# A gated recurrence on TensorE: diagonal chunk scores as whole 128 by 128 products, or as 32 by 32 blocks

## The chip, the cores and the metric

The kernel runs on one core of a Trainium2 chip. The core has a matrix engine (TensorE, "PE" in the profile, with its weight loads shown apart as "PEld"), a vector engine (DVE), an activation engine (ACT), a general engine (POOL) and a queue engine that issues transfers (SP). They run side by side and wait for one another through semaphores. SBUF is the working memory, with 128 partitions; PSUM is the memory that TensorE writes, also with 128 partitions, from which DVE and ACT copy out.

The metric is the device time of one execution in microseconds. Less is better.

## The reference

Two layers of a decoder trunk over 1024 positions of width 1024, in float32. Layer 0 mixes positions by sliding-window attention, layer 1 by a gated linear recurrence with 8 heads of key width 128 and value width 128. The change is in layer 1 alone. There, with a query `qi`, a key `ki`, a value `vi` and a log forget gate `gi` for each position and head, and chunks of 32 positions:

```python
def step(S, inp):
    qi, ki, vi, gi = inp
    b = jnp.cumsum(gi, axis=2)
    b_last = b[:, :, -1:, :]
    o_inter = jnp.einsum('bhck,bhkv->bhcv', qi * jnp.exp(b), S)
    diff = b[:, :, :, None, :] - b[:, :, None, :, :]
    decay = jnp.exp(jnp.where(causal, diff, -jnp.inf))
    scores = jnp.einsum('bhtk,bhtsk->bhts', qi, decay * ki[:, :, None, :, :])
    o_intra = jnp.einsum('bhts,bhsv->bhtv', scores, vi)
    S_new = S * jnp.exp(b_last)[:, :, 0, :, None] + jnp.einsum(
        'bhck,bhcv->bhkv', ki * jnp.exp(b_last - b), vi)
    return S_new, o_inter + o_intra
```

A query position sees the keys of its own chunk up to itself, each decayed by the gates between the two, and everything older through the state `S`. Before the recurrence a projection makes q, f (the gate) and the values, after it comes a norm, a second gate z and an output projection.

## The kernel before

The kernel doesn't keep the reference's chunk of 32. It treats 128 positions at a time, so there are 8 chunks a head, and builds a score matrix `sc` of 128 keys (on the partitions) by 128 queries for each chunk. The state is carried from chunk to chunk only. `scores_block(h, Q, F, K)` makes the scores of one head, with arrays of 128 features on the partitions and 1024 positions along the row:

- L753 to L781 prepare, on DVE and POOL: two scans (L757, L758) make running products of the gates inside blocks of 16 positions; from them come `U` and `V`, the queries and keys scaled so that their product within a block of 32 positions is right, and `X` and `Y` (the arrays Q and K themselves, further scaled) for the parts off the diagonal.
- L783 to L788 make the diagonal parts. For each of the 8 chunks TensorE multiplies all 128 keys of `V` by all 128 queries of `U`, four chunks in one PSUM tile of tag "s". A copy with a mask (L788) then takes over, out of each 128 by 128 product, only the four 32 by 32 blocks on the diagonal and of these only the keys that are not later than the query. `sc` was set to zero once, by `zeros`, so the rest stays zero.
- L789 to L797 make the parts between neighbouring blocks of 32: 16 matmuls of 32 keys by 32 queries, whose outputs stand at partitions 0 to 31 and 64 to 95 of one more PSUM tile, and two copies on ACT.
- L798 to L810 scale `X` and `Y` further (L802 on DVE, L803 on POOL) and make the parts between the two halves of a chunk: 8 matmuls of 64 by 64, and one copy on ACT.

`rec(h)` calls it and goes on: transposes of `Y` (L824), the state's increments (L830) and its update on DVE (L834, L836), then the outputs `sc` times values (L843) and queries times state (L845).

Everything in float32 leaves two records on TensorE for each matmul of the program. The big products of the projections go through `product` (L189), which makes three passes over operands that have been split into a high and a low part; their weights come from HBM through `fetch` and are split on ACT (L154) and DVE (L155) as buffers come free (`advance`, `used`).

The order of the units is `plan` in `mixer1` (L873, L874): the projections for head h+1 or h+2 stand before the recurrence of head h, so that TensorE has them to do while DVE and POOL prepare the scores. The order of the instructions on each engine is then laid out when the program is built, by a scheduler that follows an estimated time line (L1037), so the work of a head may be cut and interleaved with that of its neighbours. PSUM tiles of one tag share two buffers (`pp`, L100). `scs` holds two score matrices, one for even and one for odd heads. The other form, `scores_tree`, is for gates that are too small; it is not run with these inputs.

Of the kernel before, what the change touches and what calls it, by code (L numbers as in the profile page):

```python
# [12 lines left out]
F32 = mybir.dt.float32  # L13
# [10 lines left out]
P = 128  # L24
# [30 lines left out]
M_L, M_D, M_N = 2 * P, 2 * P + 7 * 64, 3 * P + 7 * 64  # L55
# [34 lines left out]
def emit(tc, I, out):  # L90
    nc = tc.nc
    v = InOrder(tc, nc.vector)
    from contextlib import ExitStack
    top = ExitStack()
    with top:
# [4 lines left out]
        pp = top.enter_context(tc.tile_pool(name="ps", bufs=2, space=PSUM))  # L100
# [7 lines left out]
        msk = const.tile([P, M_L], U8, name="msk")  # L108
# [557 lines left out]
        def mixer1(fast, vo, rp):  # L666
# [6 lines left out]
            msk = rp.tile([P, M_N - M_L], U8, name="msk")  # L673
# [74 lines left out]
            def scores_block(h, Q, F, K):  # L748


                sc = scs[h % 2]

                v.tensor_copy(F1[:, ::16], F[:, :T:16])  # L753
                nc.gpsimd.memset(F[:, :T:16], 0.0)
                U = rp.tile([P, T], F32, tag="U", name="U")
                V = rp.tile([P, T], F32, tag="V", name="V")
                v.tensor_tensor_scan(U, F[:, :T], F1, 0.0, op0=ALU.mult, op1=ALU.add)  # L757
                v.tensor_tensor_scan(V[:, ::-1], F[:, T:0:-1], E1[:, ::-1], 0.0, op0=ALU.mult, op1=ALU.add)  # L758
                v.tensor_tensor(Q, Q, U, op=ALU.mult)
                v.tensor_tensor(K, K, V, op=ALU.mult)  # L760

                def blk(a, n):
                    return a.rearrange("p (b two n) -> p b two n", two=2, n=n)

                tt = rp.tile([P, 6, 32], F32, tag="tt", bufs=2, name="tt")
                t32, t64, t128 = tt[:, 4, :], tt[:, 5, :16], tt[:, 5, 16:24]
                e1, e2, r1, r2 = (tt[:, i, :].unsqueeze(2).to_broadcast([P, 32, 16]) for i in range(4))
                for i in range(2):
                    v.tensor_copy(tt[:, i, :], U[:, 16 * i + 15::32])
                v.reciprocal(tt[:, 2:4, :], tt[:, 0:2, :])  # L770
                v.tensor_tensor(t32, tt[:, 0, :], tt[:, 1, :], op=ALU.mult)
                for a, b in ((t64, t32), (t128, t64)):
                    bv = b.rearrange("p (b two) -> p b two", two=2)
                    v.tensor_tensor(a, bv[:, :, 0], bv[:, :, 1], op=ALU.mult)
                Q2, K2, M2, N2 = blk(Q, 16), blk(K, 16), blk(U, 16), blk(V, 16)
                v.tensor_tensor(M2[:, :, 0, :], Q2[:, :, 0, :], r1, op=ALU.mult)
                nc.gpsimd.tensor_copy(M2[:, :, 1, :], Q2[:, :, 1, :])
                nc.gpsimd.tensor_copy(N2[:, :, 0, :], K2[:, :, 0, :])
                v.tensor_tensor(N2[:, :, 1, :], K2[:, :, 1, :], r2, op=ALU.mult)
                v.tensor_tensor(Q2[:, :, 1, :], Q2[:, :, 1, :], e1, op=ALU.mult)  # L780
                nc.gpsimd.tensor_tensor(K2[:, :, 0, :], K2[:, :, 0, :], e2, op=ALU.mult)  # L781
                X, Y = Q, K
                for b4 in range(2):  # L783
                    ps = pp.tile([P, 4, P], F32, tag="s", name="pss")
                    for i in range(4):
                        cs = slice((b4 * 4 + i) * P, (b4 * 4 + i + 1) * P)
                        nc.tensor.matmul(ps[:, i, :], V[:, cs], U[:, cs], start=True, stop=True)  # L787
                    v.copy_predicated(sc[:, b4 * 4:b4 * 4 + 4, :], msk[:, M_D - M_L:].unsqueeze(1).to_broadcast([P, 4, P]), ps)  # L788
                ps = pp.tile([P, 8, 64], F32, tag="s", name="pss")  # L789
                for c in range(8):  # L790
                    for j in range(2):
                        o = c * P + 64 * j
                        nc.tensor.matmul(ps[64 * j:64 * j + 32, c, :32], Y[:, o:o + 32], X[:, o + 32:o + 64],  # L793
                                         start=True, stop=True)
                for j in range(2):
                    o = 64 * j
                    nc.scalar.activation(sc[o:o + 32, :, o + 32:o + 64], ps[o:o + 32, :, :32], AF.Copy)  # L797
                for n, tot in ((32, t32), (64, t64)):  # L798
                    Xv, Yv = blk(X, n), blk(Y, n)
                    nb = T // (2 * n)  # L800
                    tv = tot.rearrange("p (b two) -> p b two", two=2)
                    v.tensor_tensor(Xv[:, :, 1, :], Xv[:, :, 1, :], tv[:, :, 0:1].to_broadcast([P, nb, n]), op=ALU.mult)  # L802
                    nc.gpsimd.tensor_tensor(Yv[:, :, 0, :], Yv[:, :, 0, :], tv[:, :, 1:2].to_broadcast([P, nb, n]),  # L803
                                            op=ALU.mult)
                    if n == 32:
                        ps = pp.tile([P, 8, 64], F32, tag="s", name="pss")
                        for c in range(8):
                            nc.tensor.matmul(ps[:64, c, :], Y[:, c * P:c * P + 64], X[:, c * P + 64:(c + 1) * P],  # L808
                                             start=True, stop=True)
                        nc.scalar.activation(sc[:64, :, 64:], ps[:64], AF.Copy)  # L810
                return sc, X, Y, t128

            def rec(h):
                vt = vo[h // 4]
                hc = slice((h % 4) * P, (h % 4 + 1) * P)
                ins = (qfk[h, 0], qfk[h, 1], qfk[h, 2])
                sc, X, Y, tot = scores_block(h, *ins) if fast else scores_tree(*ins)
                yn = rp.tile([P, 8, P], F32, tag="yn", name="yn")
                S = rp.tile([P, 8, P], F32, tag="S", name="S")
# [221 lines left out]
```

## Time and profile before

| What | us |
|---|---|
| median of 3 runs | 926.09 (924.61 to 927.68) |
| the profiled execution, device time | 928.78 |
| the profiled execution, span from first to last instruction | 927.0 |
| first and last start of the 128 by 128 products (L787) in it | 482.9 and 736.7 |

The profile is of one execution. A line of its groups gives the source line, the engine, the operation, the tile written and the tiles read, the shape, the count, then the time that the group was busy, the mean of one in ns, and the idle time of the engine just before. A line of its time line gives start, duration, engine, source line, operation, tiles, shape and count; neighbours of one group are merged. A line of the busy times by windows gives, for each engine, its busy time and in brackets how many instructions touch the window. For TensorE the ends of matmuls are modelled and overlap, so what one costs is read from the distance of starts.

### The profile page before, as it was taken

What the parts mean: (1) busy time and instruction counts of PE and PEld (TensorE: products, weight loads), DVE (VectorE), ACT (ScalarE), POOL (GpSimd) and SP (SyncE); (2) the same over time, 40 slices, a digit from 0 to 9 for tenths busy, and PEclk for the clock granted to TensorE, in tenths of its full rate; (3) what the DMA queues carried; (4) which work ended last, traced back from release to release, by engine and by line L of the source; (5) the groups of instructions that cost most, each with busy time, mean ns of one, the idle gap of its engine ahead of it and who ended that gap; (6) DMA issues with size and microseconds to landing.
All of it is one profiled execution on the core that took longest, in us unless ns stands there. A gap on an engine that the chain in (4) does not pass through costs nothing.

```text
span 927.0 us, 13290 instructions
## 1 busy us (share of the span) xinstructions
PE 900.5 (97%) x4830; PEld 754.3 (81%) x4830; DVE 545.9 (59%) x895; ACT 374.5 (40%) x958; POOL 350.1 (38%) x506
## 2 busy tenths in 40 slices
PE   6989999999999999999999999999999999999996
PEld 4768888888887788878888888888888888888885
DVE  6859898777885535762276864227775835252233
ACT  6425667666656332543322331323233234242211
POOL 5503455667787203330153531114433633220011
PEclk9998999999999999999999999999999999999998
DMA  7454364512312223541210010121111002022053
GB/s 283 135 154 144 109 180 141 160 55 65 92 52 60 91 67 135 176 136 37 89 58 28 20 46 1 53 62 35 35 46 47 1 1 81 11 82 101 24 181 118
DMA packets 53252, 78.56 MB, mean 85 GB/s; under 512 B 4760, under 2 KB 24984, under 8 KB 53176
## 3 DMA queue, kind: packets, MB, share of 16 engines
q1 hardware_dynamic: 53032, 77.51, 26.9%
q8 instruction: 40, 0.66, 0.3%
q14 instruction: 36, 0.29, 0.1%
q10 hardware_dynamic: 144, 0.10, 0.1%
HBM read 58.89 MB, written 16.88 MB: 82 GB/s over the span
## 4 chain that ended last, share of the span: by engine, by line
PE 76%; POOL 8%; DVE 5%; issue 5%; DMA 3%; ACT 2%; SPq 0%; POOLq 0%; ACTq 0%; DVEq 0%
PE psmm L189 62%; POOL rstd L217 2%; PE pso L843 2%; PE pss L787 2%; PE pso L845 1%; PE psk L830 1%; PE pss L514 1%; PE pss L515 1%; POOL ms L215 1%; PE pst L535 1%; POOL mY L546 1%; PE pss L808 1%; POOL mY L549 1%; DMA sinT<-csd 1%; PE pst L824 1%
## 5 line engine op out<-in xcount | busy, mean ns | idle before, releaser
L189 PE MATMUL psmm<-acth,whi 128*128 128x512 f32 x528 | 209.6, 397 | 2.0 <-DVE th L474 1.1
L189 PE MATMUL psmm<-acth,wlo 128*128 128x512 f32 x528 | 208.8, 395 | 0.2 <-POOL wlo L155 0.2
L189 PE MATMUL psmm<-actl,whi 128*128 128x512 f32 x528 | 208.6, 395 | 0.0
L189 PE MATMUL psmm<-whi,acth 128*128 128x512 f32 (+1 forms) x520 | 202.5, 391 | 1.1 <-DVE y L616 0.6
L189 PE MATMUL psmm<-wlo,acth 128*128 128x512 f32 (+1 forms) x520 | 201.3, 388 | 0.0
L189 PE MATMUL psmm<-whi,actl 128*128 128x512 f32 (+1 forms) x520 | 201.3, 388 | 0.0
L155 DVE TENSOR_TENSOR wlo<-wraw,whi 128x512 fp32r<-128x512 f32 x126 | 92.3, 745 | 108.6 <-ACT whi L154 103.7
L189 PEld LDWEIGHTS psmm<-acth,whi 128*128 128x128 f32 x528 | 99.6, 189 | 22.5 <-DVE th L474 2.2
L189 PEld LDWEIGHTS psmm<-acth,wlo 128*128 128x128 f32 x528 | 99.6, 189 | 19.8 <-POOL wlo L155 0.6
L189 PEld LDWEIGHTS psmm<-whi,acth 128*128 128x128 f32 x520 | 97.7, 188 | 21.4 <-DVE y L616 0.9
L189 PEld LDWEIGHTS psmm<-actl,whi 128*128 128x128 f32 x528 | 99.7, 189 | 18.3
L189 PEld LDWEIGHTS psmm<-whi,actl 128*128 128x128 f32 x520 | 97.7, 188 | 20.3 <-DVE actl L593 0.6
L189 PEld LDWEIGHTS psmm<-wlo,acth 128*128 128x128 f32 x520 | 97.8, 188 | 19.0
L154 ACT ACTIVATE whi<-wraw 128x512 fp32r<-128x512 f32 x112 | 70.3, 631 | 87.6 <-PE psmm L189 67.3
L529 ACT ACTIVATE sm<-sm,st 128x129 f32<-128x129 f32 x128 | 50.1, 394 | 53.4 <-DVE st L527 53.4
L698 POOL TENSOR_SCALAR gate<-gate,lbt 128x512 f32<-128x512 f32 x16 | 15.5, 970 | 127.1 <-ACT gate L696 127.1
L217 POOL TENSOR_TENSOR rstd<-ms,nhalf 128x1 f32<-128x1 f32 (+1 forms) x48 | 42.7, 889 | 3.8
L904 DVE TENSOR_TENSOR y<-psmm,wpost 128x512 f32<-128x512 f32 (+1 forms) x17 | 11.2, 660 | 52.4 <-ACT jk L903 49.7
L546 POOL TENSOR_SCALAR_AFFINE_SELECT mY<-pT 64x256 fp32r<-64x256 f32 x56 | 29.3, 523 | 32.2 <-ACT pT L538 27.1
L803 POOL TENSOR_TENSOR kk<-kk,tt 128x512 f32<-128x512 f32 x16 | 24.9, 1558 | 34.5 <-PE pss L793 28.6
L514 PE MATMUL pss<-KH,QS 128*128 128x256 f32 (+1 forms) x128 | 33.4, 288 | 3.7 <-DMA QS<-qd 3.7
L903 ACT ACTIVATE jk<-psmm 128x512 f32<-128x512 f32 (+1 forms) x17 | 9.7, 573 | 65.7 <-PE psmm L189 65.7
(225 smaller groups left out, 1465.5 us busy)
## 6 DMA issues: line engine op xcount, KB each, us to landing
wraw<-in_w SPq DMA_DIRECT2D x132, 256.0 KB
QS<-qd SPq DMA_DIRECT2D x16, 512.0 KB
xr<-in_x SPq DMA_DIRECT2D x8, 512.0 KB
x1d<-xn SPq DMA_DIRECT2D x8, 512.0 KB
xr<-x1d SPq DMA_DIRECT2D x8, 512.0 KB
out_dram<-xn SPq DMA_DIRECT2D x16, 256.0 KB
xh<-in_x SPq DMA_DIRECT2D x4, 512.0 KB
qd<-qh SPq DMA_DIRECT2D x8, 256.0 KB
```

The source lines that it names most:

```text
L154: nc.scalar.activation(hi, raw, AF.Copy)
L155: W["split_ins"][i] = (nc.gpsimd if on_pool else v).tensor_tensor(lo, raw, hi.bitcast(F32), op=ALU.subtract)
L189: nc.tensor.matmul(ps, a, b, start=(k == 0 and i == 0), stop=(k == NK - 1 and i == 2))
L217: W["rstd"] = keep(nc.gpsimd.tensor_tensor(r, m, nhalf[:, :width], op=ALU.pow))
L514: nc.tensor.matmul(ps[:, i, :nkk], q, KH[:, g, k0:k0 + nkk], start=True, stop=False)
L529: nc.scalar.activation(sm[:, h, :], sm[:, h, :], AF.Exp, bias=nm[:, h:h + 1], scale=0.125, accum_out=dn[:, h:h + 1])
L546: nc.gpsimd.affine_select(mY[r, :, :64], src[64:, :, :64].bitcast(F32), [[0, 4], [-1, 64]], ALU.is_gt, 0.0, base=0, channel_multiplier=1)
L698: nc.gpsimd.tensor_scalar(dst, dst, ol, lb, op0=ALU.mult, op1=ALU.add)
L787: nc.tensor.matmul(ps[:, i, :], V[:, cs], U[:, cs], start=True, stop=True)
L803: nc.gpsimd.tensor_tensor(Yv[:, :, 0, :], Yv[:, :, 0, :], tv[:, :, 1:2].to_broadcast([P, nb, n]), op=ALU.mult)
L843: nc.tensor.matmul(po[:, i, :], sc[:, c, :], vt[:, c, hc], start=True, stop=(c == 0))
L904: v.tensor_tensor(y[:, c0:c1], ps, wpost[:, c * 512 + c0:c * 512 + c1], op=ALU.mult)
```

## The change

The whole products of the diagonal are replaced by blocks. For each chunk `c` and each block of 32 positions at offset `o`, one matmul takes the 32 keys of `V` and the 32 queries of `U` at the same positions, and writes its 32 by 32 result to PSUM at partitions `o` to `o + 31`, in the columns of chunk `c`. All 32 results of a head fit one tile of 128 partitions by 8 by 32. Then four copies with a mask, one for each group of 32 partitions, take all 8 chunks over into `sc`.

```diff
                 X, Y = Q, K
-                for b4 in range(2):
-                    ps = pp.tile([P, 4, P], F32, tag="s", name="pss")
-                    for i in range(4):
-                        cs = slice((b4 * 4 + i) * P, (b4 * 4 + i + 1) * P)
-                        nc.tensor.matmul(ps[:, i, :], V[:, cs], U[:, cs], start=True, stop=True)
-                    v.copy_predicated(sc[:, b4 * 4:b4 * 4 + 4, :], msk[:, M_D - M_L:].unsqueeze(1).to_broadcast([P, 4, P]), ps)
+
+                ps = pp.tile([P, 8, 32], F32, tag="s", name="psd")
+                for c in range(8):
+                    for o in range(0, P, 32):
+                        cs = slice(c * P + o, c * P + o + 32)
+                        nc.tensor.matmul(ps[o:o + 32, c, :], V[:, cs], U[:, cs], start=True, stop=True)
+                for o in range(0, P, 32):
+                    r = slice(o, o + 32)
+                    mk = msk[r, M_D - M_L + o:M_D - M_L + o + 32]
+                    v.copy_predicated(sc[r, :, r], mk.unsqueeze(1).to_broadcast([32, 8, 32]), ps[r])
                 ps = pp.tile([P, 8, 64], F32, tag="s", name="pss")
```

A head has 32 matmuls where it had 8, with a quarter of the columns on either side; four masked copies of 32 by 256 where it had two of 128 by 512; and three PSUM tiles of tag "s" where it had four. The new matmuls write the tile `psd`. Everything else is as before; the lines behind it move down by four.

## The prediction

> **What bounds the kernel now.** I read the page first: the busy times, then the chain of work that ended last, by engine and by line.
>
> ```profile
> PE 900.5 (97%) x4830; PEld 754.3 (81%) x4830; DVE 545.9 (59%) x895; ACT 374.5 (40%) x958; POOL 350.1 (38%) x506
> PE 76%; POOL 8%; DVE 5%; issue 5%; DMA 3%; ACT 2%; SPq 0%; POOLq 0%; ACTq 0%; DVEq 0%
> PE psmm L189 62%; POOL rstd L217 2%; PE pso L843 2%; PE pss L787 2%; PE pso L845 1%; PE psk L830 1%; PE pss L514 1%; PE pss L515 1%; POOL ms L215 1%; PE pst L535 1%; POOL mY L546 1%; PE pss L808 1%; POOL mY L549 1%; DMA sinT<-csd 1%; PE pst L824 1%
> ```
>
> TensorE carries three quarters of that chain, and the line to be changed, L787, is 2% of it. A busy TensorE may still be waiting inside, so I asked for the stage itself: the busy times by windows through the recurrence, and the waits of PE from 419 to 836 us.
>
> ```profile
> core 0: us, PE busy (x) PEld busy (x) DVE busy (x) ACT busy (x) POOL busy (x), PEclk, DMA share, GB/s
> 480.00:520.00 40.00, 40.00 (x286) 34.15 (x285) 28.08 (x40) 12.53 (x32) 14.54 (x17) 1.00 0.17 54
> ...
> 720.00:770.00 50.00, 50.00 (x319) 42.67 (x318) 27.94 (x43) 11.30 (x34) 23.21 (x19) 1.00 0.00 1
> 770.00:836.00 66.00, 66.00 (x335) 55.43 (x335) 29.30 (x40) 26.72 (x57) 16.68 (x15) 1.00 0.22 70
> ```
>
> Between 480 and 836 us PE is busy in every microsecond, at a granted clock of 1.00. The wait view for that stretch has no row at all, and the next engine, DVE, is busy 28.08 of 40 us where it is fullest. So a microsecond that TensorE loses or gains in this stage moves the end by a microsecond, as long as nobody new makes it wait. Nothing but PE time and PE waits has to be priced.
>
> **The change part by part: the matmuls.** Each head now makes 8 whole 128 by 128 products at L787. How long such a block holds TensorE is read from the starts in the time line, because the modelled ends overlap.
>
> ```profile
> 482.41 0.39 PE L189 MATMUL psmm<-acth,whi 128*128 128x512 f32 x1
> 482.63 0.39 PE L189 MATMUL psmm<-actl,whi 128*128 128x512 f32 x1
> 482.86 0.39 PE L189 MATMUL psmm<-acth,wlo 128*128 128x512 f32 x1
> 483.09 1.95 PE L787 MATMUL pss<-U,V 128*128 128x128 f32 x16
> 484.79 0.48 PE L189 MATMUL psmm<-acth,whi 128*128 128x512 f32 x1
> 485.11 0.39 PE L189 MATMUL psmm<-actl,whi 128*128 128x512 f32 x1
> ```
>
> The 8 products are 16 records: a float32 matmul leaves two. Two plain projection slots take 482.86 - 482.41 = 0.45 us. From the last plain start before the block to the second after it are 485.11 - 482.86 = 2.25 us, so the block costs 2.25 - 0.45 = **1.80 us** a head.
>
> The new block has 4 x 8 = 32 matmuls, 64 records, each of 32 stationary columns and 32 moving columns over 128 rows. That form is already in this trace: L793 has it, 16 matmuls a head, with outputs that alternate between partitions 0 and 64.
>
> ```profile
> 489.21 0.39 PE L189 MATMUL psmm<-actl,whi 128*128 128x512 f32 x1
> 489.53 0.70 PE L793 MATMUL pss<-qf,kk 128*32 128x32 f32 x32
> 490.16 0.50 PE L189 MATMUL psmm<-acth,wlo 128*128 128x512 f32 x1
> 490.50 0.39 PE L189 MATMUL psmm<-acth,whi 128*128 128x512 f32 x1
> ...
> 496.42 0.39 PE L189 MATMUL psmm<-acth,wlo 128*128 128x512 f32 x1
> 496.73 1.15 PE L808 MATMUL pss<-qf,kk 128*64 128x64 f32 x16
> 497.81 0.50 PE L189 MATMUL psmm<-acth,whi 128*128 128x512 f32 x1
> 498.14 0.39 PE L189 MATMUL psmm<-actl,whi 128*128 128x512 f32 x1
> ```
> ```profile
> 489.52:489.55 0.03, 0.02 (x2) 0.02 (x2) 1.00 0.00 0
> L808 PE MATMUL pss<-qf,kk 128*64 128x64 f32 x128 | 9.2, 225 | 0.0
> L793 PE MATMUL pss<-qf,kk 128*32 128x32 f32 x256 | 6.1, 198 | 0.0
> ```
>
> L793's block costs 490.50 - 489.21 - 0.45 = 0.84 us. Its records start over 0.70 - 0.20 (the last one's own 198 ns) = 0.50 us, so 0.84 - 0.50 = 0.34 us is a fixed price of leaving and entering the full-width form. L808 gives the same: 1.72 - 0.45 = 1.27 us, of which 1.15 - 0.22 = 0.93 us are starts, again 0.34 us beside them. In L808 all outputs stand at the same partitions, and a record takes 0.93/15 = 62 ns for 64 columns, so 31 ns for 32, alone. In L793 a record comes every 0.50/32 = 16 ns. That is twice as often as one alone could: **the two groups of output partitions run side by side**, and the window of 30 ns at the start of the block holds two starts already.
>
> The new block goes round four groups, partitions 0, 32, 64 and 96. No row shows four at once, so its price is bounded from both sides. If all four run side by side, 64 records are 16 rounds of four at 31 ns, 0.50 us, and the block costs 0.84 us, a gain of 0.96 us a head. If never more than two run, it is 64 x 16 ns = 1.00 us, a cost of 1.34 us and a gain of 0.46 us. If none overlap, 64 x 31 ns = 1.98 us, a cost of 2.32 us and a loss of 0.52 us. I take the first, with 0.02 us for the later starts in a round: **0.94 us a head, 7.5 us for eight heads**. My reason is that a group seems to wait for nothing but its own previous record (31 ns alone, two records in 31 ns with two groups).
>
> The Trainium skill, page "TensorE: Matmul & The Clock Gate", section "Wait — 56ns, not 53.3ns?", speaks against the change: it says that matmuls never start closer than about 25 ns, however few columns they have. The 16 ns above don't agree. By that rule the block would cost 64 x 25 ns + 0.34 us = 1.94 us, 0.14 us a head more than now. Part 3 of the same page has groups of output columns starting some 4 ns apart and three of them 2.38 times as fast as one; carried over to four (estimate: 2.38/3 x 4 = 3.2 times) it would give 31/3.2 x 64 = 0.62 us, a gain of 0.84 us a head.
>
> **Cuts of the block.** The order on the engines is laid out when the program is built, and it cuts blocks where another head's work is ready. One such cut of L793 shows the price.
>
> ```profile
> 516.48 0.39 PE L845 MATMUL pso<-S,qf 128*128 128x128 f32 x2
> 516.80 0.31 PE L793 MATMUL pss<-qf,kk 128*32 128x32 f32 x6
> 517.04 0.49 PE L843 MATMUL pso<-o,sc 128*128 128x128 f32 x2
> 517.37 0.39 PE L845 MATMUL pso<-S,qf 128*128 128x128 f32 x2
> ```
>
> From 516.48 to 517.37 are 0.89 us. Two pairs of 128-column records would take 2 x 2 x 0.111 = 0.45 us (1.80/16 = 0.11 us each), and 6 records at 16 ns another 0.10 us, so the cut costs 0.34 us more, the fixed price again. The old L787 blocks are cut once in three heads (at 543, 713 and 734 us, below), and that cost nothing, because the neighbours had the same width.
>
> ```profile
> 543.41 1.56 PE pss L787 x14
> 713.66 1.56 PE pss L787 x14
> 734.33 0.81 PE pss L787 x6
> ```
>
> The same three cuts would now cost 3 x 0.34 = 1.0 us. In the first two of these heads the rest of L787 stands directly before L793; where the whole new block does, one fixed price is saved, up to 0.7 us. I take 0.5 us for both together, between 0.3 (all of it saved) and, for twice the cuts and no neighbours, 2.0.
>
> **The copies.** Two copies with a mask over 128x512 become four over 32x256.
>
> ```profile
> L522 DVE COPY_PREDICATED sm<-msk,pss 128x256 f32<-128x256 uint8 x64 | 26.8, 444 | 0.7 <-PE pss L515 0.5
> L788 DVE COPY_PREDICATED sc<-msk,pss 128x512 f32<-128x512 uint8 x16 | 11.8, 737 | 5.4 <-PE pss L787 5.4
> L797 ACT ACTIVATE sc<-pss 32x256 f32<-32x256 f32 x16 | 6.0, 372 | 21.0 <-PE pss L793 20.8
> L518 ACT ACTIVATE sm<-pss 128x256 f32<-128x256 f32 x56 | 20.0, 381 | 0.8 <-PE pss L515 0.3
> ```
>
> On ACT, 32 partitions cost the same as 128 (372 against 381 ns), so I price the new copy by the row of 128x256: 4 x 0.444 = 1.78 us against 2 x 0.737 = 1.47 us, **0.3 us more DVE time a head**, 2.4 us in all. It could be no more than 4 x 0.737 = 2.9 us. The old first copy waits for four products (8 records, 0.9 us), the new ones for all 32 matmuls (0.5 us of starts, 1.0 us if only two run at once), so they begin about when they do now, or some 0.3 us later.
>
> ```profile
> 484.33 1.49 DVE L788 COPY_PREDICATED sc<-msk,pss 128x512 f32<-128x512 uint8 x2
> 485.71 0.21 DVE L753 COPY F<-gate 128x64 f32<-128x64 f32 x1
> 486.23 2.29 DVE L757 TENSOR_TENSOR_SCAN U<-gate,F 128x1024 f32<-128x1024 f32 x1 [0.31 <-POOL gate L754]
> L843 PE MATMUL pso<-o,sc x64: 271/275/377, 515.1 to 634.6; 128*128 128x128 f32 x64
> ```
>
> Queued behind the copies on DVE is the next head's preparation (L753, L757), which TensorE needs only some 25 us later, at that head's L787 (511 us). The scores themselves are first read by L843 at 515 us. The cover is PE's projections; without it the copies would cost at most those 2.4 us. A head also takes three buffers of tag "s" in place of four, and its L793 no longer has to wait for a copy of the same head; neither was waited for, so I price that at zero. No DMA is added or moved. Work of PE that ends 7 us earlier wants its weights earlier; the DMA share is 0.00 from 720 to 770 us, because all buffers are full, so there is room.
>
> The sum: -7.5 + 0.5 = **-7.0 us**. It is made against the profiled execution, 928.78 us with a span of 927.0 us; that is 2.7 us above the median of the runs shown, and I carry the difference over to the median: 926.1 - 7.0 = **919.1 us**.
>
> **The rivals.** (1) TensorE runs only two groups at once, or looks ahead only far enough for two: 8 x 0.46 = 3.7, less 0.5, so 922.9 us; with a look-ahead between, 920 to 922. For it: two is all the trace shows. Against it: nothing in the 31 ns rounds looks full, two starts fit into 30 ns. (2) Slower: neighbouring groups exclude each other. The only pair shown, 0 and 64, isn't adjacent; the new order always steps to a neighbour, so every record would run alone: 8 x 0.52 + 0.5 = 4.7 us, 930.8 us. It decides from 1.80 - 0.34 = 1.46 us for 64 starts, 23 ns a record. (3) Each step to another group has a price of its own, so that a record comes midway between the 16 ns of two groups and the 31 ns of one alone, every 23.5 ns: 1.50 + 0.34 = 1.84 us a block, 8 x 0.04 + 0.5 = 0.8 us, 926.9 us, no change that can be told. The mean of 16 ns in L793, which changes its group at each matmul, speaks against it. The Trainium skill's floor of 25 ns ("TensorE: Matmul & The Clock Gate", "Wait — 56ns, not 53.3ns?") lies near this price; the trace goes below it. (4) The change does what it says, but the new order of the program cuts the blocks often: at 0.34 us a cut, 14 cuts eat 4.7 of the 7.5 us and leave 2.8; three are there now. That gives 923.3 us. Nothing here speaks for so many.
>
> **How the numbers follow.** My forecast has 0.58, rival 1 0.25, rival 2 0.06, rival 3 0.04, rival 4 0.07. The likeliest time is 919.1 us. The range goes from 917.0 (all four groups, no cut, neighbours joined, and a microsecond of scatter) to 924.0, past rival 1 and rival 4; it leaves out rivals 2 and 3 and some tails. About 0.3%, 2.8 us, is what a measurement of this kernel can tell from no change. Faster by more is the forecast and three quarters of rival 1, 0.76; slower by more is rival 2 and a tail of rival 3, 0.07; the rest, 0.17, is within.
>
> **What would show it.** In the changed kernel's time line the new matmuls should be 64 records a head whose starts take about 0.52 us, with PE still busy throughout 480 to 760 us. 1.0 us would be rival 1, 1.5 us rival 3, 2.0 us rival 2. More than six stretches of them beyond eight would be rival 4. The masked copies should take about 0.44 us each. I'm wrong in the premise if PE gets a wait in the recurrence, or if the last stage starts earlier and yet the end doesn't move.

## The result and the profile after

The changed kernel took 919.97 us (median of 6 runs, 919.27 to 922.27) against 926.06 us before (6 runs, 924.61 to 927.68). The ratio is 0.9938, with a 95% interval of 0.9923 to 0.9954: about 0.6%, 6.1 us, faster. Forecast were 919.1 us and a gain of 7.0 us.

From the page of the profile after, the busy times and the chain by engine:

```profile
span 917.5 us, 14082 instructions
PE 891.1 (97%) x5214; PEld 744.8 (81%) x5214; DVE 551.2 (60%) x911; ACT 373.7 (41%) x958; POOL 342.1 (37%) x506
...
PE 72%; POOL 9%; DVE 7%; issue 5%; DMA 3%; ACT 2%; SPq 0%; POOLq 0%; ACTq 0%; DVEq 0%
```

PE's busy time fell by 9.4 us and the span by 9.5 us, though the medians differ by only 6.1 us. The chains of the two traces tell the rest. First before, then after; columns are start, duration, what:

```profile
419.08 64.17 PE psmm L189 x283
483.25 1.78 PE pss L787 x16
```
```profile
415.96 64.17 PE psmm L189 x283
480.13 0.72 PE psd L788 x51
480.85 0.55 PE pss L797 x31
```

The long stretch of projections that ends at the first block of the recurrence starts 3.1 us earlier in the profile after, ahead of anything that changed. That part is scatter of the single executions (the changed kernel's own executions differ by up to 2.4 us there). From the start of this stretch to the end of the span are 927.0 - 419.08 = 507.9 us before and 917.5 - 415.96 = 501.5 us after: **6.4 us** less. I call this the tail. Two more executions of the changed kernel, profiled beside the experiments, have tails of 501.7 and 501.9 us, so it is a steadier measure than the span; it is used below beside the ratios. What scatter it has sits at its end: from the start of TensorE's last product (L189) to the end of the span are 8.6, 8.7 and 9.0 us in the three traces of the changed kernel, and as little as 8.0 us in others below. Up to that start the stage takes 918.25 - 419.08 = 499.2 us before, and 493.0, 493.1 and 493.0 us after, **6.1 to 6.2 us** less; tails that differ by about 1 us are compared by this instead.

The first block after, in PE's time line:

```profile
479.29 0.39 PE L189 MATMUL psmm<-acth,whi 128*128 128x512 f32 x1
479.51 0.39 PE L189 MATMUL psmm<-actl,whi 128*128 128x512 f32 x1
479.74 0.39 PE L189 MATMUL psmm<-acth,wlo 128*128 128x512 f32 x1
480.06 0.79 PE L788 MATMUL psd<-U,V 128*32 128x32 f32 x64
480.70 0.70 PE L797 MATMUL pss<-qf,kk 128*32 128x32 f32 x32
481.33 0.50 PE L189 MATMUL psmm<-acth,whi 128*128 128x512 f32 x1
481.66 0.40 PE L189 MATMUL psmm<-actl,whi 128*128 128x512 f32 x1
```
```profile
480.05:480.09 0.04, 0.03 (x4) 0.03 (x5) 1.00 0.00 0
```

64 records start over 0.79 - 0.20 = 0.59 us, 9 ns each. The window row under it (busy time of the new matmuls alone) holds four starts in 30 ns: all four groups of output partitions run side by side. And the neighbour blocks (now L797) follow directly, without full-width work between. Both together cost 481.66 - 479.74 - 0.45 = 1.47 us, where the old kernel paid 1.80 + 0.84 = 2.64 us in two places. I call such an unbroken run of narrow (32-column) records between full-width work a stretch.

The masked copies and the waits of PE in the recurrence, after:

```profile
L792 DVE COPY_PREDICATED sc<-msk,psd 32x256 f32<-32x256 uint8 x32 | 14.1, 442 | 7.0 <-PE psd L788 5.7 <-PE pss L797 0.8
PE psd L788 <- DVE tt L774: 0.9, 1, 0.9
PE psmm L189 <- DVE qf L690: 0.2, 1, 0.2
```

A copy takes 442 ns, as priced. The waits are new: PE had none in this stage before.

### The profile page after: what moved, and what is told of

It is laid out like the page before. It is cut to its first block, busy times and chain, and to the rows that moved or that the text cites. A ratio compares the mean times of both kernels' runs of the same rounds, so it can differ in the third digit from the quotient of the medians.

```text
span 917.5 us, 14082 instructions
## 1 busy us (share of the span) xinstructions
PE 891.1 (97%) x5214; PEld 744.8 (81%) x5214; DVE 551.2 (60%) x911; ACT 373.7 (41%) x958; POOL 342.1 (37%) x506
## 4 chain that ended last, share of the span: by engine, by line
PE 72%; POOL 9%; DVE 7%; issue 5%; DMA 3%; ACT 2%; SPq 0%; POOLq 0%; ACTq 0%; DVEq 0%
PE psmm L189 59%; POOL rstd L217 2%; PE psk L834 1%; PE pso L847 1%; PE pss L514 1%; PE pss L515 1%; POOL ms L215 1%; PE pso L849 1%; PE pst L535 1%; POOL mY L546 1%; POOL mY L549 1%; DMA sinT<-csd 1%; PE pss L812 1%; PE pst L828 1%; PE pst L861 1%
## 5 line engine op out<-in xcount | busy, mean ns | idle before, releaser
L189 PE MATMUL psmm<-acth,whi 128*128 128x512 f32 x528 | 210.0, 398 | 1.6 <-DVE th L474 1.1
L189 PE MATMUL psmm<-acth,wlo 128*128 128x512 f32 x528 | 208.1, 394 | 0.2 <-POOL wlo L155 0.2
L189 PE MATMUL psmm<-actl,whi 128*128 128x512 f32 x528 | 208.2, 394 | 0.0
L189 PE MATMUL psmm<-whi,acth 128*128 128x512 f32 (+1 forms) x520 | 202.4, 391 | 1.0 <-DVE y L616 0.6
L189 PE MATMUL psmm<-wlo,acth 128*128 128x512 f32 (+1 forms) x520 | 201.2, 388 | 0.0
L189 PE MATMUL psmm<-whi,actl 128*128 128x512 f32 (+1 forms) x520 | 201.2, 388 | 0.0
L189 PEld LDWEIGHTS psmm<-acth,whi 128*128 128x128 f32 x528 | 99.6, 189 | 21.9 <-DVE th L474 2.2
L189 PEld LDWEIGHTS psmm<-acth,wlo 128*128 128x128 f32 x528 | 99.5, 189 | 19.9 <-POOL wlo L155 0.6
L189 PEld LDWEIGHTS psmm<-whi,acth 128*128 128x128 f32 x520 | 97.7, 188 | 21.2 <-DVE th L474 0.9
L189 PEld LDWEIGHTS psmm<-actl,whi 128*128 128x128 f32 x528 | 99.7, 189 | 18.4
L189 PEld LDWEIGHTS psmm<-whi,actl 128*128 128x128 f32 x520 | 97.7, 188 | 20.3 <-DVE actl L593 0.8
L189 PEld LDWEIGHTS psmm<-wlo,acth 128*128 128x128 f32 x520 | 97.8, 188 | 19.1
L698 POOL TENSOR_SCALAR gate<-gate,lbt 128x512 f32<-128x512 f32 x16 | 17.7, 1108 | 121.8 <-ACT gate L696 121.8
L546 POOL TENSOR_SCALAR_AFFINE_SELECT mY<-pT 64x256 fp32r<-64x256 f32 x56 | 29.3, 523 | 31.8 <-ACT pT L538 26.8
L549 POOL TENSOR_SCALAR_AFFINE_SELECT mY<-pT 64x256 fp32r<-64x256 f32 x64 | 30.8, 481 | 6.0 <-ACT pT L538 1.4
```

What stands on the lines that cost most here:

```text
L189: nc.tensor.matmul(ps, a, b, start=(k == 0 and i == 0), stop=(k == NK - 1 and i == 2))
L546: nc.gpsimd.affine_select(mY[r, :, :64], src[64:, :, :64].bitcast(F32), [[0, 4], [-1, 64]], ALU.is_gt, 0.0, base=0, channel_multiplier=1)
L549: nc.gpsimd.affine_select(mY[r, :, 64:], src[:64, :, 64:].bitcast(F32), [[0, 4], [1, 64]], ALU.is_ge, 0.0, base=0, channel_multiplier=-1)
L698: nc.gpsimd.tensor_scalar(dst, dst, ol, lb, op0=ALU.mult, op1=ALU.add)
```

## The experiments

Each changes the new kernel in one place and keeps the rest.

| run | us | ratio to before | tail, us |
|---|---|---|---|
| changed kernel, again | 921.97 | 0.9938 (0.9922 to 0.9955) | 501.7 |
| group by group | 928.56 | 1.0013 (1.0003 to 1.0024) | 509.2 |
| two groups | 922.07 | 0.9952 (0.9937 to 0.9966) | 502.6 |
| blocks twice | 927.26 | 1.0000 (0.9990 to 1.0010) | 507.5 |
| copies twice | 926.92 | 0.9989 (0.9979 to 0.9998) | 507.3 |
| half the copies | 919.80 | 0.9928 (0.9907 to 0.9949) | 500.4 |
| two tiles | 929.29 | 1.0025 (1.0008 to 1.0042) | 509.8 |
| uncut | 919.61 | 0.9932 (0.9917 to 0.9948) | 501.4 |
| changed kernel, again | 922.11 | 0.9938 (0.9924 to 0.9952) | 501.9 |
| uncut, copies as before | 922.23 | 0.9948 (0.9935 to 0.9962) | 501.8 |

The kernel before had medians of 926.5 to 927.6 us beside them. In "copies twice" the chain doesn't pass through the stretch by which the tail is taken, so its start is read from PE's time line, 418.82 us there and 416.03 us in the changed kernel.

> The changed kernel once more, beside the experiments. About 920.0 us, 0.9938 of the kernel before, by every theory.

> The changed kernel once more, beside the next one. Ratio to the kernel before 0.9938, by every theory.

Both came out at 0.9938.

**Is it the rotation over groups, or the size alone?** Group by group:

```diff
-                for c in range(8):
-                    for o in range(0, P, 32):
+                for o in range(0, P, 32):
+                    for c in range(8):
```

> The same 32 matmuls a head, but all eight of one group of output partitions before the next group. Theory (groups run side by side, each waits 31 ns for its own last record): the 64 records a head take 1.0 us where the queue of TensorE reaches into the next group, up to 64 x 31.7 ns = 2.0 us where it does not, in place of 0.6 us; the kernel takes 923 to 931 us. Rival (small products are cheap by their size, the order doesn't matter): 920 us, starts over 0.6 us as before.

Its first block in PE's time line:

```profile
482.00 1.82 PE L788 MATMUL psd<-U,V 128*32 128x32 f32 x61
483.63 0.22 PE L797 MATMUL pss<-qf,kk 128*32 128x32 f32 x2
483.66 0.20 PE L788 MATMUL psd<-U,V 128*32 128x32 f32 x1
```

61 starts in 1.82 - 0.20 = 1.62 us, 27 ns each, three times as long as in the rotating order; the tail is 7.3 to 7.7 us longer, and the whole gain is gone. Size alone buys nothing. Two groups at a time:

```diff
-                for c in range(8):
-                    for o in range(0, P, 32):
+                for half in range(2):
+                    for c in range(8):
+                        for o in (32 * half, 32 * half + 64):
```

> The same 32 matmuls a head, the groups at partitions 0 and 64 first in turns, then those at 32 and 96. Stretches as in the changed kernel, 16. Theory (a group waits 31 to 32 ns for its own last record, so two groups give a record every 16 ns): 1.0 us of starts a head in place of 0.6, 8 x 0.42 = 3.4 us more than the changed kernel, ratio about 0.9975. Rival (groups are not what makes it quick): ratio 0.994, starts over 0.6 us.

```profile
481.53 0.39 PE L189 MATMUL psmm<-acth,wlo 128*128 128x512 f32 x1
481.85 1.02 PE L789 MATMUL psd<-U,V 128*32 128x32 f32 x58
482.68 0.22 PE L798 MATMUL pss<-qf,kk 128*32 128x32 f32 x2
...
483.64 0.39 PE L189 MATMUL psmm<-actl,whi 128*128 128x512 f32 x1
```

58 starts take 1.02 - 0.20 = 0.82 us, 14 ns each. With the neighbours the stretch costs 483.64 - 481.53 - 0.45 = 1.66 us against 1.47. The direction is as expected, the size is not: up to TensorE's last product 1.4 to 1.5 us more in place of 3.4. The interval of the ratio doesn't tell this run from the changed kernel; the starts do. One reason is in the rows: records of L798 start among the last ones of L789, and the trace shows the same where the second pair follows the first.

**What sets the pace of a long block?** Each block made twice:

```diff
-                for c in range(8):
+                for c in list(range(8)) * 2:
```

> Each diagonal block of a head is made twice into the same place, so 128 records a head instead of 64. In the changed kernel's trace the first 32 records or so of a block come four in 32 ns, 8 ns each, the later ones every 16 to 17 ns. Theory (the first ones stood in the queue already, later ones come as fast as instructions reach TensorE): the further 64 records cost 64 x 16.7 ns = 1.07 us a head, 8.6 us in all, and with two cuts more (0.7 us) the kernel takes 929 us. Rival (the slow end is an effect of the end of a block; the four groups alone set the pace): 64 x 8 ns = 0.51 us a head, 4.1 + 0.7 us, 925 us.

```profile
481.93 1.32 PE L788 MATMUL psd<-U,V 128*32 128x32 f32 x128
```

128 starts take 1.32 - 0.20 = 1.12 us; the second 64 cost 0.53 us here, 8 ns each. The theory of a slow supply of instructions falls; the rival's 4.8 us is near the 5.6 to 6.0 us by which the tail grew (507.5 against 501.5 to 501.9). Over all eight heads the starts grew by 5.0 us, and two more stretches make 0.7 us. I had misread the end of a block, where starts come in pairs (one or two ns apart, the next pair 15 ns later), as single starts 16 ns apart.

**Do the copies lie under TensorE's work?** Twice, and half (the copies of the groups at 64 and 96 are left out):

```diff
-                for o in range(0, P, 32):
+                for o in list(range(0, P, 32)) * 2:
                     r = slice(o, o + 32)
```

> The four masked copies of a head are made twice, 4 x 0.442 = 1.77 us more of DVE a head, 14.1 us in all. Theory (DVE's copies lie under TensorE's work): nothing but two cuts more of the narrow blocks, 0.7 us: 920 to 922 us, and TensorE still busy throughout the recurrence but for a microsecond. Rival (DVE has become the bound in the recurrence, since it is busy 31 to 33 of 40 us there): up to 934 us, with waits of TensorE on DVE.

```diff
-                for o in range(0, P, 32):
+                for o in range(0, 64, 32):
                     r = slice(o, o + 32)
```

> The masked copies of the groups at partitions 64 and 96 are left out, so half of the diagonal scores are missing; DVE has 2 x 0.442 = 0.88 us less a head, 7.1 us in all. Stretches as in the changed kernel, 16. Theory (DVE is close to its limit in the recurrence, where doubled copies cost 5 of 14 us, but the changed kernel pays for it with 1.1 us of waits at most): 0 to 1.1 us less than the changed kernel, ratio 0.9925 to 0.994. Rival (the masked copies hold TensorE up by more than the waits show): 2 to 3 us less, ratio 0.991.

Doubled, the copies cost 0.9989 - 0.9938 = 0.5%, 4.7 us by the ratio and 5.4 to 5.8 us by the tail, of the 14 us added: more than the theory, less than the rival. PE's waits on DVE and one place of its time line, copies twice:

```profile
PE psmm L189 <- DVE qf L690: 3.9, 4, 1.4
PE psd L788 <- DVE V L779: 0.7, 1, 0.7
```
```profile
526.99 0.39 PE L189 MATMUL psmm<-acth,wlo 128*128 128x512 f32 x1
528.03 0.69 DVE L690 TENSOR_TENSOR qf<-psmm,sg 128x512 f32<-128x512 f32 x1
528.77 0.50 PE L189 MATMUL psmm<-acth,whi 128*128 128x512 f32 x1 [1.40 <-DVE qf L690]
```

The projections stop because a PSUM buffer of theirs is emptied by L690 on DVE, which stands in DVE's queue behind the longer work. Halved, the copies bring 0.1%, which the intervals don't tell from nothing. The tail is 500.4 against 501.5 to 501.9 us, 1.1 to 1.5 us less, but about half of that lies behind TensorE's last product; up to it the gain is 492.4 against 493.0 to 493.1 us, 0.6 to 0.7 us. PE's waits in the recurrence, half the copies:

```profile
PE pst L828 <- POOL kk L807: 0.4, 1, 0.4
PE psmm L189 <- DVE qf L690: 0.2, 1, 0.2
```

The wait of 0.9 us for L774 is gone, and one of 0.4 us for POOL is new. DVE's part in the changed kernel is small, and it is not zero.

**What does a cut cost?** Two tiles, so that the neighbour blocks must wait for a buffer again:

```diff
+                for b4 in range(2):
+                    ps = pp.tile([P, 4, 32], F32, tag="s", name="psd")
...
-                    v.copy_predicated(sc[r, :, r], mk.unsqueeze(1).to_broadcast([32, 8, 32]), ps[r])
+                        v.copy_predicated(sc[r, b4 * 4:b4 * 4 + 4, r], mk.unsqueeze(1).to_broadcast([32, 4, 32]), ps[r])
```

> The same 32 matmuls a head, but into two PSUM tiles of four chunks each, with eight masked copies of 32x128 in place of four of 32x256, so that the neighbour blocks have to wait for a buffer again. In the program's order the narrow float32 blocks then stand in 25 stretches between full-width work, where the changed kernel has 16. Theory (each stretch costs 0.34 us of leaving and entering the full-width form, whatever is in it): 9 x 0.34 = 3.1 us more than the changed kernel, ratio to the kernel before about 0.997. Rival (the stretches cost nothing, the blocks alone set the time): the changed kernel's ratio, 0.994.

The tail grew by 8.3 us, not by 3.1. Waits of PE, the busy times by windows (the granted clock is the third figure from the end) and a piece of the time line, two tiles:

```profile
PE psd L789 <- DVE V L779: 3.4, 1, 3.4
PE pss L813 <- DVE qf L807: 0.4, 1, 0.4
```
```profile
728.20:730.83 2.63, 0.47 (x2) 0.15 (x1) 2.63 (x3) 0.59 (x1) 2.63 (x2) 1.00 0.00 0
730.84:732.04 1.20, 0.00 (x0) 0.02 (x1) 1.20 (x3) 0.00 (x0) 1.20 (x2) 0.50 0.00 0
732.05:737.65 5.60, 5.60 (x44) 4.48 (x45) 3.10 (x7) 0.00 (x0) 2.43 (x2) 0.50 0.00 0
737.67:740.00 2.33, 2.33 (x17) 1.70 (x16) 0.00 (x0) 0.00 (x0) 0.00 (x0) 1.00 0.00 0
```
```profile
734.94 0.63 PE L189 MATMUL psmm<-whi,acth 128*128 128x512 f32 x1
735.37 0.63 PE L189 MATMUL psmm<-wlo,acth 128*128 128x512 f32 x1
```

3.8 us are waits on DVE, whose eight copies cost more than four (19.0 us against 14.1 in all); the changed kernel has 1.1 us of waits itself, so this adds 2.7 us. After the long one the clock is 0.50 for 5.6 us of work, and a projection slot takes 0.43 us in place of 0.23: eleven slots of them are 2.2 us. Some 8.3 - 2.7 - 2.2 = 3.4 us are left for ten more stretches (nine of 32-column blocks, and one block of L813 is cut too), 0.34 us each. As a remainder of an experiment that did more than was meant, that would be weak; but the price also stands in the time line by itself:

```profile
639.97 0.39 PE L189 MATMUL psmm<-acth,wlo 128*128 128x512 f32 x1
640.29 0.27 PE L789 MATMUL psd<-U,V 128*32 128x32 f32 x8
640.49 0.50 PE L189 MATMUL psmm<-acth,whi 128*128 128x512 f32 x1
640.82 0.39 PE L189 MATMUL psmm<-actl,whi 128*128 128x512 f32 x1
```

From 639.97 to 640.82 are 0.85 us; less 0.45 for the two slots and 0.27 - 0.20 = 0.07 for the starts, 0.33 us remain, for a stretch of 8 records as for one of 96 (1.47 - 1.14 = 0.33 us in the changed kernel's first, where 1.14 us lie between the first start and the last). By the same reckoning each of the ten stretches before and fourteen of the sixteen after cost 0.32 to 0.33 us; PE waited in the other two.

**A version without cuts.** The diagonal and the neighbour blocks get priority:

```diff
-                ps = pp.tile([P, 8, 32], F32, tag="s", name="psd")
+                with hp():
+                    ps = pp.tile([P, 8, 32], F32, tag="s", name="psd")
...
```

> The diagonal and the neighbour blocks with their copies go ahead of other ready work, so that in the program's order all 48 narrow matmuls of a head stand in one stretch: 8 stretches in place of 16. Theory of the stretches: 8 x 0.34 = 2.7 us less than the changed kernel, and the 0.9 us wait of the last head may go or stay: ratio to the kernel before about 0.991. Rival (stretches cost nothing, or DVE's copies, now earlier, hold the next preparation up): 0.994 or more.

> As in the uncut version, all 48 narrow matmuls of a head stand in one stretch (8 stretches, the changed kernel has 16), but only the matmuls go ahead of other ready work; the masked copies keep their place. In the uncut version TensorE waited 1.1 us on DVE for the state and 1.1 us for the last head's preparation. Theory (the uncut version gave its 2 us back because the copies, ahead on DVE, held the state up): these waits go down to about 1 us, and the ratio is 0.9925 or less, 1 to 2 us below the changed kernel. Rival (the waits come from DVE being full there, wherever the copies stand): as the changed kernel, 0.993 to 0.994, with 2 us of waits.

There are 8 stretches, as meant, and neither version is measurably faster than the changed kernel. Waits of PE in the recurrence, uncut:

```profile
PE psd L789 <- DVE tt L774: 1.1, 1, 1.1
PE pso L848 <- DVE S L841: 1.1, 3, 0.6
PE psmm L189 <- DVE qf L690: 0.2, 1, 0.2
```

The second version has the same three rows with the same times, so the place of the copies is not the reason; its theory falls and the rival's time holds, while its reason, a full DVE, isn't tested by itself. By 0.34 us a stretch 2.7 us should have come. By these rows the waits grew by 1.3 us over those of the changed kernel. The modelled ends hide a part of each wait, though: read from the distances of starts, as the blocks are, PE loses about 3.3 us at them in the uncut version and 1.3 us in the changed kernel, 2.0 us more. The starts of the narrow records add 0.3 us. Some 0.4 us of gain should be left; up to TensorE's last product 492.8 us against 493.0 to 493.1 show 0.2 to 0.3 us.

## Why the prediction was right, point by point

- **TensorE bounds the stage.** Right but for 1.1 us: the tail fell with PE's work, and PE is busy throughout the recurrence but for two waits on DVE. The prediction had named any wait of PE there as a sign that its premise fails; to that extent it did.
- **The groups run side by side, four at once.** Right. This was the step without a row, and it carried the result: 0.59 us of starts against a forecast of 0.52, no other case nearer (1.0, 1.5, 2.0). The first block was 0.07 us dearer than forecast. Over all stretches the 32-column records take 9.1 us from first start to last, where the old L793 alone took 4.1, so the new matmuls take 5.0 us in place of 8 x 0.52 = 4.2: the term was 0.8 us too small. The two experiments on the order show that the rotation is the cause. The Trainium skill's floor of 25 ns between starts ("TensorE: Matmul & The Clock Gate", "Wait — 56ns, not 53.3ns?") doesn't hold here, at 9 ns; the estimate from Part 3 of that page, 0.62 us, was close.
- **Cuts.** Half right. I counted three cuts more and perhaps two joined neighbours, and "priced at zero" that L793 no longer waits for a copy of its own head. That freed buffer is what lets the neighbour blocks follow at once: the last part of every new block has L797 directly behind it, whole in seven heads and its first two records in the last one; with two tiles, which take the buffer back, that happens in one head only. Against this stand more cuts than I thought: the new matmuls are in 14 stretches, six beyond eight, just as many as the prediction allowed before it would speak of rival 4. With L797 the narrow blocks are in 16 stretches, where the old L793 alone was in 10. I had counted 8 x 0.34 us for the new blocks and 0.5 us for cuts and joins, 3.2 us; six more stretches at 0.33 us are 2.0 us, 1.2 us on the good side.
- **Copies.** Their duration was right, their cover not quite: new waits of 1.1 us, and half the copies gone brings 0.6 to 0.7 us back.
- The sum with these sizes is -7.0 + 0.8 - 1.2 + 1.1 = -6.3 us, against 6.1 us less by the medians and 6.4 us by the tail. The errors offset each other in part; the near hit of the sum owes that much to luck.
- **The rivals.** Two groups only, exclusion of neighbouring groups, and a price for each step of group are all ruled out by the four starts in 30 ns and by the 9 ns a record. The many cuts came in part, six in place of the fourteen of rival 4, and the joined neighbours paid for them.

## What to carry to other kernels

If only small blocks of a matmul's result are used, make the blocks alone, but give consecutive matmuls different groups of output partitions: the rotation is the gain, and in the wrong order the same small products cost as much as the whole ones. Keep narrow work together, since leaving and entering the full-width form costs a fixed time, 0.33 us here however short the stretch. Where PE and DVE are both nearly full, look at which DVE instructions empty PE's buffers before giving DVE more.

## What the runs showed of the hardware beyond that

TensorE starts matmuls out of program order when their groups are free: in the group-by-group run two records of L797, which stand behind all of L788 in the program and write to partitions 0 and 64, start at 483.63 us, before a record of L788's last group (partition 96) at 483.66 us. In the two-tile run a wait of PE of 3.38 us was followed by 5.6 us of work at a granted clock of 0.50, so a long wait costs more than itself. The windows show the clock fall at about 730.83 us, 2.2 us into the wait, and come back near 737.66 us. The Trainium skill ("TensorE: Matmul & The Clock Gate", "What's actually happening") has the same two rates: half after an idle window of about 3.4 us, full after a busy one of that length. This case agrees with the rates, but the fall came before PE had been idle for 3.4 us. The waits of 0.9 to 1.4 us in the other runs left the clock at 1.00. And most of the scatter between executions of one kernel, up to 2.4 us in the profiles of the changed kernel, lies ahead of the recurrence: the long stretch of projections starts at 415.96, 415.98 and 418.36 us, while the tails agree within 0.4 us and the times up to TensorE's last product within 0.1 us.
